# Feed-forward weights in 8 KB runs per partition, read back by transposes of every fourth column

## The chip, the cores and the metric

One core of one Trainium2 chip runs the whole program. The metric is the device time of one execution in microseconds; lower is better. The kernel before was run three times, and one more execution was profiled. TensorE (PE) multiplies, with its weight loads shown apart (PEld); VectorE (DVE), ScalarE (ACT) and GpSimd (POOL) work on tiles; SyncE (SP) only issues DMAs, which 16 DMA engines carry out.

## What is computed

The reference is a two-layer backbone over 1024 tokens of width 1024: layer 0 mixes the tokens with a gated DeltaNet and pooling, layer 1 with a short gated convolution, and each layer ends with a mixture of 16 experts in which every expert chooses its 128 tokens. The change touches that part alone:

```python
aff = softmax(h @ router)                        # (n, 16)
gate, idx = top_k(aff.T, cap)                    # cap = 2 * 1024 / 16 = 128 tokens per expert
xg = h[idx]                                      # (16, 128, 1024)
hid = silu(xg @ w_gate) * (xg @ w_up)            # w_gate, w_up: (16, 1024, 512)
y = (hid @ w_down) * gate[..., None]             # w_down: (16, 512, 1024)
out = zeros_like(h).at[idx].add(y)
```

All arrays are float32.

## The kernel before

A product of full precision is made of three TensorE products: both operands are split into a high part (fp32r) and a rest, and high by high, high by low and low by high are summed (`mm3`, lines 140 to 142). So each granule of weights, 1 MB in 128 partitions of 2048 floats, goes through three steps. SyncE fetches it into one of eight `raw` buffers (line 71), ScalarE casts it to `whi` (line 88, in one piece in these stages), and VectorE subtracts to `wlo` (line 89), which frees the raw buffer for the next fetch. The split buffers `whi` and `wlo` come from a rotation of several pools; a cast waits until TensorE has read what was there.

`granules` (line 380) gives the order in which an expert's weights are fetched: gate and up of the first 512 input rows, gate and up of the other 512, then two granules of `w_down`, each with all 512 rows and half of the columns. In DRAM a row of each granule is 512 floats, and partition p takes rows p, 128 + p, 256 + p and 384 + p: four runs of 2 KB. `fetch`, `prefetch` and `weight` keep fetched and split granules in order, some ahead of their use.

`experts` (line 405) is the loop over the 16 experts. For each it gathers the rows of the expert three places later (`gather`: GpSimd's indirect DMA, line 359, after counts on ScalarE and TensorE, lines 353 and 354; ScalarE then copies the affinity out of the gathered rows, line 362). It transposes the next expert's rows, eight TensorE transposes of 128 columns each into two PSUM tiles (`transposed`, line 372), and splits the results into `xh` and `xl`. Then come 48 gate and up products of 512 columns, Silu on ScalarE (line 434), the product with up on VectorE (line 435), four transposes of the hidden values (line 438) and their split into `hh` and `hl`. The down projection has 16 products with `hh` (line 452), granule after granule, and 8 with `hl` (line 455), four per granule, after each four of which VectorE scales a half of `y` out of PSUM (line 457). GpSimd adds `y` to the tokens' rows by an indirect DMA (line 462); the last expert's rows are added by one-hot products in `sums`.

In a transpose the data is the operand that TensorE loads as weights, and the identity matrix streams through.

The tile framework orders each engine's instructions by a schedule of its own when the kernel is built, with the marks `high_priority` and `issue_after`; within an engine they then run in that order. The loads of `ada_w` early in the program and in layer 1 use other helpers, which the change does not touch; a part of them has 8 KB per partition in one run.

Of the kernel before, what the change touches and what calls it, by code (L numbers as in the profile page):

```python
# [9 lines left out]
F32 = mybir.dt.float32  # L10
# [10 lines left out]
P = 128  # L21
D = 1024
# [4 lines left out]
NE = 16  # L27
# [7 lines left out]
class Cycle:  # L35
# [6 lines left out]
    def next(self):  # L42
        self.at += 1
        return self.pools[(self.at - 1) % len(self.pools)]
# [15 lines left out]
class Weights:  # L60
# [6 lines left out]
    def fetch(self, src, shape):  # L67

        t = self.raw.tile([P, self.size], F32, tag="raw", name=self.co.name("raw"))[:, : math.prod(shape)]
        t = t.rearrange("p (a b) -> p a b", a=shape[0])  # L70
        self.loaded = self.co.nc.sync.dma_start(t, src).ins
        return t
# [131 lines left out]
    nc.vector.memset(co.ones16, 1.0)  # L204


class Moe:


# [155 lines left out]
    def transposed(self, xg, pool, ps):  # L365

        co = self.co
        halves = []
        for half in range(2):
            pt = ps.tile([P, 512], F32, tag="tr", name=co.name("pt"))  # L370
            for k in range(4):
                self.nc.tensor.transpose(
                    pt[:, k * P : (k + 1) * P], xg[:, (4 * half + k) * P : (4 * half + k + 1) * P], co.ident
                )
            hi, lo = (pool.tile([P, 4, P], F32R, tag=tag, name=co.name(tag), bufs=3) for tag in ("xh", "xl"))
            co.split(hi.rearrange("p k t -> p (k t)"), lo.rearrange("p k t -> p (k t)"), pt)
            halves.append((hi, lo))
        return halves

    def granules(self):  # L380

        w_gate, w_up, w_down = self.w
        for e in range(NE):
            for half in range(2):
                for w in (w_gate, w_up):
                    yield w[e, half * 512 : (half + 1) * 512, :].rearrange("(k p) f -> p k f", p=P)
            for half in range(2):
                yield w_down[e, :, half * 512 : (half + 1) * 512].rearrange("(k p) f -> p k f", p=P)

    def fetch(self, weights, n):  # L390
        for _ in range(n):
            self.fetched.append(weights.fetch(next(self.stream), (4, 512)))

    def prefetch(self, weights, n, lo_engine=None, in_raw=False):
        for _ in range(n):
# [9 lines left out]
    def experts(self, pool, weights, ps, raws, before_last, scatter_last):  # L405

        co, nc = self.co, self.nc
        rows = [self.gather(e, pool, ps) for e in range(3)]
        ahead = self.transposed(rows[0][2], pool, ps)
        with co.tc.issue_after(self.routed):
            self.prefetch(weights, min(4, 6 - len(self.ahead)), nc.gpsimd)
        with co.tc.issue_after(self.placed):
            self.prefetch(weights, 6 - len(self.ahead), nc.vector)
        for e in range(NE):
            (idx, aff, _), halves = rows.pop(0), ahead
            if e + 3 < NE:  # L420
                rows.append(self.gather(e + 3, pool, ps))
            if rows:
                with co.tc.high_priority(100):
                    ahead = self.transposed(rows[0][2], pool, ps)
            lo_engine = nc.vector if e == NE - 1 else None
            acts = [ps.tile([P, 512], F32, tag="gu", name=co.name("gu")) for w in range(2)]
            for half, (hi, lo) in enumerate(halves):
                for pa in acts:
                    g = self.weight(weights, lo_engine)
                    for k in range(4):  # L430
                        co.mm3(pa, (hi[:, k, :], lo[:, k, :]), (g[0][:, k, :], g[1][:, k, :]), half == k == 0, half == 1 and k == 3)
            with co.tc.high_priority(100):
                sg = pool.tile([P, DE], F32, tag="sg", name=co.name("sg"), bufs=1)
                nc.scalar.activation(sg, acts[0], AF.Silu)
                nc.vector.tensor_tensor(sg, sg, acts[1], op=ALU.mult)
                pt = ps.tile([P, 512], F32, tag="tr", name=co.name("pt"))
                for k in range(4):
                    nc.tensor.transpose(pt[:, k * P : (k + 1) * P], sg[:, k * P : (k + 1) * P], co.ident)
                hh = pool.tile([P, 4, P], F32R, tag="hh", name=co.name("hh"), bufs=1)
                hl = pool.tile([P, 4, P], F32R, tag="hl", name=co.name("hl"), bufs=1)  # L440
                co.split(hh.rearrange("p k t -> p (k t)"), hl.rearrange("p k t -> p (k t)"), pt)

            y = (
                pool.tile([P, ROW], F32, tag="xg", name=co.name("y"), bufs=3)[:, :D]
                if e == NE - 2 else pool.tile([P, D], F32, tag="y", name=co.name("y"), bufs=1)
            )
            down = [(self.weight(weights, lo_engine, e == NE - 1), ps.tile([P, 512], F32, tag="y", name=co.name("py"))) for half in range(2)]

            for g, py in down:
                for k in range(4):  # L450
                    for w in range(2):
                        nc.tensor.matmul(py, hh[:, k, :], g[w][:, k, :], start=k == w == 0, stop=False)  # L452
            for half, (g, py) in enumerate(down):
                for k in range(4):
                    nc.tensor.matmul(py, hl[:, k, :], g[0][:, k, :], start=False, stop=k == 3)  # L455
                sl = slice(half * 512, (half + 1) * 512)
                nc.vector.scalar_tensor_tensor(y[:, sl], py, aff, self.g2[:, sl], op0=ALU.mult, op1=ALU.mult)  # L457
            if e == NE - 1:
                xs = self.sums(idx, y, raws, pool, ps, *before_last(pool, ps))
                if not scatter_last:  # L460
                    return xs
            self.scattered = nc.gpsimd.indirect_dma_start(  # L462
                out=self.acc[:, :],
                out_offset=bass.IndirectOffsetOnAxis(ap=idx, axis=0),
                in_=y,
                in_offset=None,
                compute_op=ALU.add,
            ).ins
        return xs
# [1035 lines left out]
def hybrid_dit_kernel(stack, tc, aps):  # L1505
# [29 lines left out]
    with ExitStack() as sa:  # L1535
# [21 lines left out]
        with ExitStack() as left:  # L1557
# [40 lines left out]
            with tc.issue_after(loads[5]):  # L1598
                gs = {0: [weights.split(raw) for raw in fetch(0)]}
# [13 lines left out]
        invert = lambda h: mx.invert(h, E[h], Ys, heads, ps)  # L1613
        weave(project(0, 0))
        ahead = fetch(1)
        weave(project(0, 1), mx.decays(0, E[0], heads))
        base = []
        for h in range(H):

            gs[h + 1] = [weights.split(ahead.pop(0))]  # L1620
            weave(project(h, 2), front(h, 0), base[-3:])
            gs[h + 1] += [weights.split(raw) for raw in ahead]
            before = invert(h - 1) if h else []
            if h == H - 1:
                ada_pools.close()
                blocks = left.enter_context(pooled("base"))
                Ys += mx.inverse_buffers(blocks, 2)
            base = front(h, 2) + urgent(mx.base(h, heads if h < H - 1 else blocks, heads, nc.vector if h == H - 1 else nc.gpsimd), 300)
            if h + 1 < H:
                weave(project(h + 1, 0), front(h, 1), before[:8], ada[h][:18])  # L1630
                ahead = fetch(h + 2)
                weave(
                    project(h + 1, 1), base[:-3], before[8:] + mx.decays(h + 1, E[h + 1], heads), ada[h][18:],
                )
# [297 lines left out]
```

## Time and profile before

| what | value |
|---|---|
| median of 3 runs | 1886.85 us (1879.98 to 1890.77) |
| the profiled execution | 1879.51 us, of it span from first to last instruction 1877.7 us |
| TensorE's busy share of the span | 88% |
| VectorE, ScalarE, GpSimd | 70%, 48%, 28% |
| DMA | 443.71 MB, 236 GB/s over the span |
| mean granted TensorE clock | 0.929 of full speed |
| feed-forward stage of layer 0, experts | 730 to 1070 us |
| feed-forward stage of layer 1, experts | 1530 to 1850 us |

The profile gives an engine's busy time, not its use: products are pipelined, and a busy TensorE may still wait between products. The share of DMA is the time that packets took over 16 engines; two queues whose packets overlap on an engine can bring it over 1. The chain of waits follows the work back from the last instruction, at each step to what released it; "issue" in it is time in which an engine waited for nothing that the profile shows. A line of the profile is a line of the kernel; line 71 is every fetch of weights, lines 88 and 89 every split, lines 140 to 142 every product of three.

### The profile page before, as it was taken

What the parts mean: (1) busy time and instruction counts of PE and PEld (TensorE: products, weight loads), DVE (VectorE), ACT (ScalarE), POOL (GpSimd) and SP (SyncE); (2) the same over time, 40 slices, a digit from 0 to 9 for tenths busy, and PEclk for the clock granted to TensorE, in tenths of its full rate; (3) what the DMA queues carried; (4) which work ended last, traced back from release to release, by engine and by line L of the source; (5) the groups of instructions that cost most, each with busy time, mean ns of one, the idle gap of its engine ahead of it and who ended that gap; (6) DMA issues with size and microseconds to landing.
All of it is one profiled execution on the core that took longest, in us unless ns stands there. A gap on an engine that the chain in (4) does not pass through costs nothing.

```text
span 1877.7 us, 26055 instructions
## 1 busy us (share of the span) xinstructions
PE 1655.3 (88%) x9561; PEld 1344.1 (72%) x9561; DVE 1305.4 (70%) x1975; ACT 897.3 (48%) x1570; POOL 530.7 (28%) x549
## 2 busy tenths in 40 slices
PE   6999997979969963999898999999999559989995
PEld 2988775758868752877677677888888447867873
DVE  4637776567878884888878858433545558888896
ACT  3645332434742434878766451101122358778673
POOL 4310386571340352212121261000012412122222
PEclk7999998879989985999999999999999769999998
DMA  7426764659667964899999648423264549999995
GB/s 289 146 81 193 222 207 125 174 157 278 194 243 259 386 252 146 302 346 372 367 345 329 206 144 301 147 68 113 73 225 142 181 138 327 373 360 353 373 326 192
DMA packets 261397, 443.71 MB, mean 236 GB/s; under 512 B 46521, under 2 KB 108714, under 8 KB 257174
## 3 DMA queue, kind: packets, MB, share of 16 engines
q1 hardware_dynamic: 252198, 408.76, 62.9%
q0 software_dynamic: 9072, 33.30, 7.0%
q8 instruction: 75, 1.23, 0.3%
q14 instruction: 52, 0.43, 0.1%
HBM read 368.65 MB, written 73.35 MB: 235 GB/s over the span
## 4 chain that ended last, share of the span: by engine, by line
PE 50%; DVE 13%; DMA 7%; ACT 5%; issue 4%; SPq 2%; POOL 0%; DVEq 0%; ACTq 0%; POOLq 0%
PE py L452 5%; PE gu L141 4%; PE gu L140 4%; PE gu L142 4%; PE pin L140 4%; PE pin L141 4%; PE pin L142 4%; PE po L141 3%; PE po L142 3%; PE po L140 3%; DVE wlo L89 3%; ACT whi L88 3%; PE py L455 2%; DMA raw<-in_w_up_dram 2%; SPq L918 1%
## 5 line engine op out<-in xcount | busy, mean ns | idle before, releaser
L89 DVE TENSOR_TENSOR wlo<-raw,whi 128x2048 fp32r<-128x2048 f32 (+3 forms) x245 | 471.9, 1959 | 82.6 <-ACT whi L88 82.5
L88 ACT CAST whi<-raw 128x2048 fp32r<-128x2048 f32 (+3 forms) x271 | 420.9, 1598 | 213.5 <-PE pin L141 77.7
L140 PE MATMUL gu<-whi,xh 128*128 128x512 f32 x512 | 206.3, 407 | 13.3 <-ACT whi L88 12.4
L141 PE MATMUL gu<-wlo,xh 128*128 128x512 f32 x512 | 207.4, 406 | 6.2 <-DVE wlo L89 6.2
L142 PE MATMUL gu<-whi,xl 128*128 128x512 f32 x512 | 204.4, 403 | 0.8 <-DVE xl L135 0.8
L462 POOL DMA_INDIRECT acc<-y,idx x31 | 83.9, 2708 | 356.8 <-DVE y L457 340.9
L141 PE MATMUL pin<-h1T,whi 128*128 128x512 f32 x384 | 150.4, 393 | 0.0
L142 PE MATMUL pin<-h1T,wlo 128*128 128x512 f32 x384 | 150.0, 393 | 0.0
L140 PE MATMUL pin<-h1T,whi 128*128 128x512 f32 x384 | 149.3, 398 | 0.0
L89 POOL TENSOR_TENSOR wlo<-raw,whi 128x1024 fp32r<-128x1024 f32 (+2 forms) x26 | 80.6, 3117 | 167.1 <-ACT whi L88 167.0
L140 PEld LDWEIGHTS gu<-whi,xh 128*128 128x128 f32 x512 | 98.7, 193 | 37.8 <-ACT whi L88 14.0
L141 PEld LDWEIGHTS gu<-wlo,xh 128*128 128x128 f32 x512 | 98.6, 193 | 31.0 <-DVE wlo L89 8.8
L142 PEld LDWEIGHTS gu<-whi,xl 128*128 128x128 f32 x512 | 98.1, 192 | 23.1 <-DVE xl L135 1.1
L452 PE MATMUL py<-whi,hh 128*128 128x512 f32 x256 | 106.4, 419 | 8.1 <-ACT hh L134 8.0
L788 DVE SCALAR_TENSOR_TENSOR adsum<-raw,cs,adsum 128x512 f32<-128x512 f32 (+1 forms) x77 | 95.3, 1238 | 24.9 <-DMA raw<-in_ada_w_dram 24.4
L452 PE MATMUL py<-wlo,hh 128*128 128x512 f32 x256 | 105.1, 412 | 0.0
L353 ACT ACTIVATE oh<-places,aff 128x128 f16<-128x128 f16 x256 | 77.9, 394 | 46.9 <-DVE aff L342 46.9
L140 PE MATMUL pq<-hT,whi 128*128 128x512 f32 (+1 forms) x256 | 98.0, 383 | 1.6 <-ACT last L1082 1.0
L359 POOL DMA_INDIRECT xg<-table,idx x32 | 48.8, 1526 | 175.9 <-ACT idx L357 133.1
L142 PE MATMUL pq<-hT,wlo 128*128 128x512 f32 (+1 forms) x256 | 97.6, 381 | 0.0
L141 PE MATMUL pq<-hT,whi 128*128 128x512 f32 (+1 forms) x256 | 97.6, 381 | 0.0
L141 PE MATMUL po<-wlo,mh 128*128 128x512 f32 x224 | 90.4, 403 | 4.5 <-DVE wlo L89 4.5
(387 smaller groups left out, 3744.3 us busy)
## 6 DMA issues: line engine op xcount, KB each, us to landing
raw<-in_w_gate_dram SPq DMA_DIRECT2D x64, 1024.0 KB
raw<-in_w_up_dram SPq DMA_DIRECT2D x64, 1024.0 KB
raw<-in_w_down_dram SPq DMA_DIRECT2D x64, 1024.0 KB
raw<-in_ada_w_dram SPq DMA_DIRECT2D x32, 1024.0 KB
raw<-in_ada_w_dram SPq DMA_DIRECT2D x64, 256.0 KB
raw<-in_sc_w_in_dram SPq DMA_DIRECT2D x12, 1024.0 KB
table<-h SPq DMA_DIRECT2D x16, 520.0 KB
raw<-in_ev_w_in_dram SPq DMA_DIRECT2D x16, 512.0 KB
```

The source lines that it names most:

```text
L88: nc.scalar.copy(hi[:, part], raw[:, part])
L89: (lo_engine or e).tensor_sub(lo[:, part], raw[:, part], hi[:, part])
L140: nc.tensor.matmul(out, lhs[0], rhs[0], start=start, stop=False)
L141: nc.tensor.matmul(out, lhs[0], rhs[1], start=False, stop=False)
L142: nc.tensor.matmul(out, lhs[1], rhs[0], start=False, stop=stop)
L353: nc.scalar.activation(oh[:, t, :], co.places, AF.Sign, bias=self.before[:, t, e : e + 1])
L359: nc.gpsimd.indirect_dma_start(out=xg, out_offset=None, in_=self.table[:, :], in_offset=bass.IndirectOffsetOnAxis(ap=idx, axis=0))
L452: nc.tensor.matmul(py, hh[:, k, :], g[w][:, k, :], start=k == w == 0, stop=False)
L455: nc.tensor.matmul(py, hl[:, k, :], g[0][:, k, :], start=False, stop=k == 3)
L462: self.scattered = nc.gpsimd.indirect_dma_start(out=self.acc[:, :], out_offset=bass.IndirectOffsetOnAxis(ap=idx, axis=0), in_=y, in_offset ...
L788: nc.vector.scalar_tensor_tensor(st["sum"], raw, cs[:, k, 0:1], st["sum"], op0=ALU.mult, op1=ALU.add)
L918: mx.nc.sync.dma_start(dst, src)
```

## The change

The weights of a granule are laid out so that partition p holds neighbouring rows of DRAM: for gate and up rows 4p to 4p + 3 of the 512, for `w_down` rows 2p and 2p + 1 of 256 rows with all 1024 columns. Each partition's part is then one run of 8 KB. The products sum over partitions, so the other operand has to have the same rows in the same partitions: the transposes of the gathered rows read every fourth column of a half, those of the hidden values every second column of a half (`every`). The down projection goes over k (the four sets of 128 hidden rows), both parts of the split and both halves of the columns, with the two PSUM tiles in turn, and the last eight products over both granules for each half. The bytes, the splits and the number of products are as before.

```diff
--- before.py
+++ after.py
@@ -202,6 +202,11 @@
     nc.vector.memset(co.one16, 1.0)
     co.ones16 = c.tile([P, 1], F16, name="ones16")
     nc.vector.memset(co.ones16, 1.0)
+
+
+def every(x, n, k):
+
+    return x.rearrange("p (t k) -> p k t", k=n)[:, k, :]
 
 
 class Moe:
@@ -370,7 +375,7 @@
             pt = ps.tile([P, 512], F32, tag="tr", name=co.name("pt"))
             for k in range(4):
                 self.nc.tensor.transpose(
-                    pt[:, k * P : (k + 1) * P], xg[:, (4 * half + k) * P : (4 * half + k + 1) * P], co.ident
+                    pt[:, k * P : (k + 1) * P], every(xg[:, 4 * half * P : 4 * (half + 1) * P], 4, k), co.ident
                 )
             hi, lo = (pool.tile([P, 4, P], F32R, tag=tag, name=co.name(tag), bufs=3) for tag in ("xh", "xl"))
             co.split(hi.rearrange("p k t -> p (k t)"), lo.rearrange("p k t -> p (k t)"), pt)
@@ -383,13 +388,13 @@
         for e in range(NE):
             for half in range(2):
                 for w in (w_gate, w_up):
-                    yield w[e, half * 512 : (half + 1) * 512, :].rearrange("(k p) f -> p k f", p=P)
+                    yield w[e, half * 512 : (half + 1) * 512, :].rearrange("(p k) f -> p k f", p=P), (4, 512)
             for half in range(2):
-                yield w_down[e, :, half * 512 : (half + 1) * 512].rearrange("(k p) f -> p k f", p=P)
+                yield w_down[e, half * 256 : (half + 1) * 256, :].rearrange("(p k) f -> p k f", p=P), (2, D)
 
     def fetch(self, weights, n):
         for _ in range(n):
-            self.fetched.append(weights.fetch(next(self.stream), (4, 512)))
+            self.fetched.append(weights.fetch(*next(self.stream)))
 
     def prefetch(self, weights, n, lo_engine=None, in_raw=False):
         for _ in range(n):
@@ -435,7 +440,8 @@
                 nc.vector.tensor_tensor(sg, sg, acts[1], op=ALU.mult)
                 pt = ps.tile([P, 512], F32, tag="tr", name=co.name("pt"))
                 for k in range(4):
-                    nc.tensor.transpose(pt[:, k * P : (k + 1) * P], sg[:, k * P : (k + 1) * P], co.ident)
+                    half = sg[:, k // 2 * 256 : (k // 2 + 1) * 256]
+                    nc.tensor.transpose(pt[:, k * P : (k + 1) * P], every(half, 2, k % 2), co.ident)
                 hh = pool.tile([P, 4, P], F32R, tag="hh", name=co.name("hh"), bufs=1)
                 hl = pool.tile([P, 4, P], F32R, tag="hl", name=co.name("hl"), bufs=1)
                 co.split(hh.rearrange("p k t -> p (k t)"), hl.rearrange("p k t -> p (k t)"), pt)
@@ -444,15 +450,17 @@
                 pool.tile([P, ROW], F32, tag="xg", name=co.name("y"), bufs=3)[:, :D]
                 if e == NE - 2 else pool.tile([P, D], F32, tag="y", name=co.name("y"), bufs=1)
             )
-            down = [(self.weight(weights, lo_engine, e == NE - 1), ps.tile([P, 512], F32, tag="y", name=co.name("py"))) for half in range(2)]
-
-            for g, py in down:
+            down = [self.weight(weights, lo_engine, e == NE - 1) for half in range(2)]
+            pys = [ps.tile([P, 512], F32, tag="y", name=co.name("py")) for half in range(2)]
+            part = lambda k, w, half: down[k // 2][w][:, k % 2, half * 512 : (half + 1) * 512]
+
+            for k in range(4):
+                for w in range(2):
+                    for half, py in enumerate(pys):
+                        nc.tensor.matmul(py, hh[:, k, :], part(k, w, half), start=k == w == 0, stop=False)
+            for half, py in enumerate(pys):
                 for k in range(4):
-                    for w in range(2):
-                        nc.tensor.matmul(py, hh[:, k, :], g[w][:, k, :], start=k == w == 0, stop=False)
-            for half, (g, py) in enumerate(down):
-                for k in range(4):
-                    nc.tensor.matmul(py, hl[:, k, :], g[0][:, k, :], start=False, stop=k == 3)
+                    nc.tensor.matmul(py, hl[:, k, :], part(k, 0, half), start=False, stop=k == 3)
                 sl = slice(half * 512, (half + 1) * 512)
                 nc.vector.scalar_tensor_tensor(y[:, sl], py, aff, self.g2[:, sl], op0=ALU.mult, op1=ALU.mult)
             if e == NE - 1:
```

## Rows read from the trace of the kernel before

**Rows 1.** The page, busy time, share of the span and instructions of TensorE

```profile
PE 1655.3 (88%) x9561; PEld 1344.1 (72%) x9561; DVE 1305.4 (70%) x1975; ACT 897.3 (48%) x1570; POOL 530.7 (28%) x549
```

**Rows 2.** Table by stage: PE, PEld, DVE, ACT, POOL busy us, clock, DMA share, GB/s

```profile
730.00:1070.00 340.00, 313.67 (x1477) 248.90 (x1478) 266.68 (x195) 243.12 (x319) 66.14 (x35) 0.95 0.91 308
...
1530.00:1850.00 320.00, 305.03 (x1448) 243.75 (x1446) 262.41 (x190) 230.90 (x279) 69.78 (x30) 0.97 0.93 320
```

**Rows 3.** Line 434 in each stage: count, duration in ns, first and last start

```profile
L434 ACT ACTIVATE sg<-gu x16: 581/598/610, 756.2 to 1049.7; 128x512 f32<-128x512 f32 x16
...
L434 ACT ACTIVATE sg<-gu x16: 579/598/616, 1545.1 to 1833.4; 128x512 f32<-128x512 f32 x16
```

**Rows 4.** Chain in order of time, 855 to 1005 us: start, duration, what

```profile
856.55 0.35 PE pi L354 x8
...
906.17 0.87 PE pt L372 x8
907.05 3.75 PE py L452 x16
910.80 1.88 PE py L455 x8
```

**Rows 5.** DMA queues, 1700 to 1780 us: packets, MB, share of 16 engines

```profile
q1 hardware_dynamic: 12444, 24.71, 83.0%
q0 software_dynamic: 1272, 4.66, 21.3%
```

**Rows 6.** DMA queues, 1136 to 1140 us, then 1125 to 1133 us

```profile
DMA packets 186, 1.39 MB, mean 348 GB/s; under 512 B 16, under 2 KB 16, under 8 KB 16
...
q1 hardware_dynamic: 186, 1.39, 85.8%
...
q1 hardware_dynamic: 352, 2.62, 88.0%
```

**Rows 7.** Chain by line, 740 to 1070 us, then 1530 to 1850 us

```profile
by line: PE py L452 14.2%; PE gu L140 11.6%; PE gu L141 11.4%; PE gu L142 11.2%; issue 9.1%; ACT whi L88 7.9%; DMA raw<-in_w_up_dram 6.7%; DVE wlo L89 5.5%; PE py L455 4.3%; DMA raw<-in_w_gate_dram 3.2%; DMA xg<-table,idx 2.9%; PE pt L372 2
...
by line: PE py L452 16.9%; PE gu L141 13.4%; PE gu L142 13.2%; PE gu L140 13.0%; ACT whi L88 7.1%; DVE wlo L89 6.8%; issue 6.1%; PE py L455 5.3%; DMA raw<-in_w_gate_dram 3.3%; PE pt L372 3.3%; DMA xg<-table,idx 3.1%; DMA raw<-in_w_up_dram 2
```

**Rows 8.** Waits of TensorE, 780 to 860 us, then 1580 to 1660: us, times, longest

```profile
PE gu L141 <- DVE wlo L89: 1.6, 3, 0.7
...
PE gu L141 <- DVE wlo L89: 4.2, 3, 3.0
PE gu L140 <- ACT whi L88: 0.9, 1, 0.9
```

**Rows 9.** Waits, ScalarE's casts for split buffers, each stage

```profile
ACT whi L88 <- PE py L455: 8.0, 8, 2.7
...
ACT whi L88 <- PE py L455: 5.0, 6, 1.5
```

**Rows 10.** Waits, ScalarE for gathered rows, each stage

```profile
ACT aff L362 <- DMA xg<-table,idx: 10.4, 4, 4.1
...
ACT aff L362 <- DMA xg<-table,idx: 10.7, 5, 3.2
```

**Rows 11.** Single lines: duration in ns, min, median, max (the last: busy us, mean ns)

```profile
L372 PEld LDWEIGHTS pt<-ident,xg x256: 137/141/231, 740.4 to 1811.1; 128*128 128x128 f32 x128
...
L1268 DVE COPY base<-base x4: 1049/1078/1110, 274.6 to 453.6; 104x1024 f32<-104x1024 f32 x4
...
L1023 ACT ACTIVATE g_beta<-gates x1: 344/344/344, 111.5 to 111.5; 128x80 f32<-128x80 f32 x1
...
L1026 ACT ACTIVATE g_e<-g_u x1: 254/254/254, 111.8 to 111.8; 128x80 f32<-128x80 f32 x1
...
L1024 DVE TENSOR_TENSOR g_u<-gates,gate_par x1: 293/293/293, 110.0 to 110.0; 128x80 f32<-128x80 f32 x1
...
L1031 DVE TENSOR_TENSOR g_ld<-g_u,gate_par x1: 242/242/242, 115.5 to 115.5; 128x80 f32<-128x80 f32 x1
...
L89 DVE TENSOR_TENSOR wlo<-raw,whi 128x2048 fp32r<-128x2048 f32 x90 | 202.8, 2288 | 27.1 <-ACT whi L88 27.0
```

## The prediction

> **What bounds the kernel now.** The page comes first: TensorE is busy 88% of the span [rows 1], but that average says nothing of the two stretches that the change touches, the feed-forward stages. So the table by stage is read next [rows 2]: from 730 to 1070 us and from 1530 to 1850 us the DMA engines are 0.91 and 0.93 busy and TensorE, VectorE and ScalarE work beside them most of the time. No engine stands out, so each is costed per expert. Sixteen experts run in a stage, and their Silu instructions mark the pace [rows 3]: from the first to the last, (1049.7 - 756.2) / 15 = 19.57 us per expert in layer 0 and (1833.4 - 1545.1) / 15 = 19.22 us in layer 1.
>
> TensorE's own work per expert, from dense places of the chain [rows 4]: 16 + 8 down products (3.75 + 1.88, 0.235 each), 48 gate and up products of the same form (11.3), 12 transposes (0.87 / 8 each, 1.3), 8 one-column counts (0.35): 18.6 us. So TensorE loses 0.97 and 0.62 us per expert, (0.97 + 0.62) x 15 = 24 us in both stages together. That is the most that a perfect feed of weights could give inside them.
>
> DMA per expert: one queue carries the weights, the other the gathers and scatters. From 1700 to 1780 us [rows 5] the weights' queue spends 0.830 x 16 x 80 / 24.71 = 43.0 us of one engine per MB, that is 88 ns for each 2 KB packet; an expert's six granules (6.29 MB) take 43.0 x 6.29 / 16 = 16.9 us. The other queue adds 0.213 x 80 = 17.0 us in that stretch of 4.2 experts, 4.1 us each. Together 21.0 us, of which some overlaps (the shares sum to 1.05), so about 20: DMA is slightly slower than the 19.2 to 19.6 us at which experts pass, and lives on the granules fetched ahead. It is the tightest supplier, by a small margin over TensorE.
>
> **The change, part by part.**
>
> *Packets of 8 KB.* The same bytes go in a quarter of the packets. ScalarE's and VectorE's splits of a granule keep their size. The kernel already has 8 KB packets, in the loads of ada_w: from 1136 to 1140 us, where only 16 of 186 packets are shorter, the queue needs 0.858 x 16 x 4 / 1.39 = 39.5 us per MB, 324 ns a packet; from 1125 to 1133 us it is 0.880 x 16 x 8 / 2.62 = 43.0 [rows 6], as for 2 KB, because starting transfers are in it. I take 39.5, the fuller stretch: 8% less, 1.4 us of 16.9 per expert, and keep 0 as the other end. DMA's pace becomes about 20.0 - 1.3 = 18.7 us per expert, beside TensorE's 18.6: it no longer sets the pace alone.
>
> What that is worth is read from the waits, not from DMA's busy time. In the chain, landings of raw weights hold 6.7 + 3.2% of 340 us in layer 0 and 3.3 + 2% of 320 us in layer 1 [rows 7]: 34 + 17 = 51 us, and 8% of it is 4.1 us. Seen from TensorE, in the two stretches where those landings stand (780 to 860, 1580 to 1660 us) it waits for splits 1.6 + 4.2 + 0.9 = 6.7 us [rows 8]. The two agree; I take 6.5 us gained, with ends 0 and 24 (all that TensorE loses).
>
> *Down projection by rows.* The 24 products stay, and so does the order of need: the first eight read only the first granule (k = 0, 1), as before. What moves is when a split buffer comes free. Before, the first granule's high part was last read by the first half's four L455 products; now both halves read both granules, and it is free after the sixth of the eight: two products, 0.47 us, later. ScalarE's casts wait for exactly this, 8 + 6 times [rows 9]. Behind those casts the rest of ScalarE's queue stands, and TensorE waits for them. At most 14 x 0.47 = 6.6 us; TensorE's own waits for casts in such places are a handful, so I take five, 2.4 us lost, ends 0 and 6.6. VectorE's evacuation of y keeps its place.
>
> *Transposes of every fourth and every second column.* 8 of 12 transposes per expert read gathered rows 16 bytes apart, 4 read the hidden values 8 bytes apart. The data is the operand of the weight load, which takes 141 ns (median) for 128 contiguous columns [rows 11]. No strided read by TensorE is in this trace. The nearest rows are of other engines [rows 11]: VectorE's copy with its source 128 bytes apart takes 1078 ns for 1024 elements, 1.05 ns each, while its subtraction of contiguous columns takes 2288 ns for 2048, 1.12 ns each; that speaks for no cost. ScalarE's activation with its source 64 bytes apart takes 344 ns for 80 elements where the contiguous one takes 254: 1.1 ns more each. VectorE's addition beside it takes 293 against 242 ns. By VectorE's copy the cost is 0; by ScalarE's it is 128 x 1.1 = 144 ns for a load, and 256 transposes of fourth columns make 37 us. A gain is excluded: the load reads as many elements. I take 0, because the copy is the longest of these rows and its rate is not hidden in fixed cost, and keep 37 us as the end. The stride of 8 bytes I cost at nothing; 128 transposes at half that price would be 9 us.
>
> [...]
>
> *Sum.* -6.5 + 2.4 + 0 = -4 us. The profiled execution took 1879.5 us (span 1877.7), at the lower edge of the three runs shown, whose median is 1886.85. Four microseconds less is 1875.5 for an execution like the profiled one, and 1883 for the median, which I forecast.
>
> **Rivals.**
>
> *B, slower: weight loads of every fourth column are slow.* Place: the eight L372 loads of each expert. Four transposes follow one another at 0.11 us, less than one load's 141 ns, so a longer load cannot hide within the four; it decides as soon as it adds some 50 ns (256 x 50 ns = 13 us). Price by ScalarE's row: 37 us of TensorE, which holds 55% of the chain in layer 0 and 65% in layer 1 [rows 7], so 0.6 x 37 = 22 us, less the 4 gained: +18, 1905. For it: ScalarE's row, and a TensorE with 0.6 to 1.0 us per expert to spare. Against: VectorE's copy. Chance 0.28.
>
> *C, clearly faster: the whole loss of TensorE goes.* If weights come early enough, ScalarE and VectorE find their splits ready and work ahead, and most of the 24 us goes: 19 us less, 1868. For it: DMA is at 1.05 of its engines in the second half of both stages. Against: only 6.7 us of TensorE's waits stand where landings do; the others follow ScalarE's casts that wait for TensorE itself [rows 9], and VectorE has 267 us of work in 340 [rows 2]. It also needs strided loads at no cost. Chance 0.22.
>
> *D, slower: gathers and scatters stand behind longer packets.* A gather has 128 rows, 8 per engine. If each takes turns with a weight packet, it waits 8 x (324 - 88) ns = 1.9 us longer. ScalarE already waits for 9 of the 32 gathers, 21.1 us in all [rows 10]; 9 x 1.9 = 17 us, less the 4 gained: +13, 1900. It decides only where ScalarE arrives before the rows do; the other 23 have slack. Chance 0.08.
>
> *A, the forecast:* chance 0.42. If packets of 8 KB are no faster than 43.0 us per MB, the change does not do what it is for, and the time stays within A as well.
>
> **How the numbers follow.** About 0.5%, 9.4 us, is what a measurement of this kernel can tell from no change. A lies within it, C below, B and D above: faster 0.22, same 0.42, slower 0.36. The range goes down to C with nearly all 24 us (1863) and up to B with 0.6 of 37 and the 6.6 of the split buffers, little gained (1886.85 + 22 + 6.6, 1914 rounded down): beyond it lie strides that cost still more, and gains outside the experts. A's own range is 1878 to 1896, no change give or take 9 us.
>
> **What would show it.** Right: the weights' queue near 39.5 us per MB; L372's loads still near 141 ns and four of them in 0.44 us; fewer landings of raw in the chain; Silu to Silu 19.0 to 19.5 us. B: L372's loads far over 141 ns. C: under 18.9 us per expert. D: ScalarE's wait for xg over 21.1 us. I am wrong if the split buffers, not the feed, prove to hold ScalarE back: then casts waiting for L455 would grow well past 13 us.

## The result: 0.8% slower, and the profile after

The changed kernel takes 1903.79 us (median of five executions, 1891.63 to 1909.49), the kernel before 1886.85 us beside it: ratio 1.0086 (95% interval 1.0061 to 1.0112, in brackets below). Run once more beside other kernels it gave 1.0072 [1.0053, 1.0091]. Both lie within the forecast range and above the 1883 us that were forecast. The profiled execution took 1891.63 us (span 1889.7), the shortest of its five; the repeat's took 1896.86 (span 1895.1).

The rate of the weights' queue became what was forecast. First the page, then the table by stage, then the DMA queues from 1700 to 1780 us (packets, MB, share of 16 engines), all of the kernel after:

```profile
PE 1665.4 (88%) x9561; PEld 1358.7 (72%) x9561; DVE 1305.2 (69%) x1975; ACT 896.8 (47%) x1570; POOL 534.2 (28%) x549
...
DMA packets 187669, 443.71 MB, mean 235 GB/s; under 512 B 46521, under 2 KB 108714, under 8 KB 158870
```

```profile
730.00:1070.00 340.00, 315.93 (x1492) 253.53 (x1492) 265.47 (x199) 241.75 (x319) 70.96 (x35) 0.95 0.85 305
1530.00:1850.00 320.00, 300.25 (x1418) 242.45 (x1419) 257.65 (x182) 235.73 (x301) 67.33 (x31) 0.96 0.89 324
```

```profile
q1 hardware_dynamic: 3375, 24.52, 75.2%
q0 software_dynamic: 1152, 4.23, 20.7%
```

The weights' queue now needs 0.752 x 16 x 80 / 24.52 = 39.3 us per MB where it needed 43.0 [rows 5]; 39.5 was forecast. DMA's share of the two stages falls from 0.91 and 0.93 [rows 2] to 0.85 and 0.89. The feed is lighter, and yet the experts pass more slowly. Silu's line shows it, first of the profiled kernel after, then of the repeat (count, duration in ns, first and last start):

```profile
L439 ACT ACTIVATE sg<-gu x16: 578/599/607, 760.1 to 1054.7; 128x512 f32<-128x512 f32 x16
...
L439 ACT ACTIVATE sg<-gu x16: 585/598/610, 1550.7 to 1845.4; 128x512 f32<-128x512 f32 x16
```

```profile
L439 ACT ACTIVATE sg<-gu x16: 587/599/608, 760.6 to 1056.7; 128x512 f32<-128x512 f32 x16
...
L439 ACT ACTIVATE sg<-gu x16: 580/598/606, 1553.5 to 1851.2; 128x512 f32<-128x512 f32 x16
```

Between the first and the last Silu lie 294.6 + 294.7 = 589.3 us, in the repeat 296.1 + 297.7 = 593.8, where the kernel before has 293.5 + 288.3 = 581.8 [rows 3]: 7.5 and 12 us more, most of them in layer 1. In layer 0 the count is not quite of the same work: the changed kernel issues one expert's 16 products with `hh` (3.8 us) ahead of the last Silu, the kernel before behind it. Measured to VectorE's last addition of a one-hot product (line 503, then 511), the two stages take 326.3 and 318.9 us before, 329.3 and 325.2 after, 332.4 and 327.9 in the repeat: two executions of one kernel differ by some 3 us a stage. Another 4 us of each span's difference stand ahead of the first Silu, where the two programs are the same up to the gathers; the profiled execution of before was a quick one (1879.51 us against a median of 1886.85).

Where did the lighter feed go? The chain by line of the kernel after, 740 to 1070 and 1530 to 1850 us:

```profile
by line: PE py L460 12.9%; PE gu L140 12.6%; PE gu L142 12.1%; PE gu L141 12.0%; ACT whi L88 9.9%; issue 8.5%; DMA xg<-table,idx 4.5%; DMA acc<-y,idx 4.4%; PE py L463 3.8%; DVE wlo L89 3.8%; PE pt L377 3.4%; DMA raw<-in_w_up_dram 3.1%; DMA 
...
by line: PE py L460 15.6%; PE gu L141 15.1%; PE gu L140 14.6%; PE gu L142 14.4%; issue 6.8%; PE py L463 5.6%; DVE wlo L89 5.2%; ACT whi L88 4.9%; DMA xg<-table,idx 3.8%; PE pt L377 3.5%; DMA raw<-in_w_down_dram 2.7%; ACT oh L358 2.4%; PE pt
```

Landings of raw weights, 51 us of the two chains before [rows 7], hold 28 us now: 3.1% of 330 and 2.7% of 320 us in these rows, and 9.4 us for `w_gate` in layer 0, where the row is cut off. Gathers (xg) grew from 2.9 and 3.1% to 4.5 and 3.8%: from 19.5 to 27 us. The scatter's 4.4% (acc) was not in the chain before; it stands at the end of layer 0. ScalarE's waits tell the same (730 to 1070 us, then 1530 to 1850: us in total, times, longest):

```profile
ACT aff L367 <- DMA xg<-table,idx: 13.0, 6, 5.5
ACT whi L88 <- PE py L463: 7.6, 2, 6.8
...
ACT whi L88 <- DMA raw<-in_w_up_dram: 1.8, 1, 1.8
...
ACT aff L367 <- DMA xg<-table,idx: 13.5, 4, 6.5
...
ACT whi L88 <- PE py L463: 7.6, 7, 1.9
ACT whi L88 <- DMA raw<-in_w_up_dram: 1.3, 1, 1.3
```

For gathers it waits 26.5 us (28.5 in the repeat) where it waited 21.1 [rows 10], and the longest waits are 5.5 and 6.5 us where they were 4.1 and 3.2. For split buffers it waits 15.2 where it waited 13.0 [rows 9]. These two are the suspects.

The gathers themselves land later. Median time from issue to landing, 790 to 1040 us, for the kernel before, for one with gate and up alone in 8 KB runs (`packets_stride4` below), and for the kernel after:

```profile
DMA to landing us min/median/max: 7.0/7.8/9.3
```

```profile
DMA to landing us min/median/max: 7.2/9.0/11.5
```

```profile
DMA to landing us min/median/max: 8.4/10.2/11.1
```

With more of the weights in long packets, the other queue's rows land later: 7.8, 9.0, 10.2 us. In the second stage it is 8.2, 8.9 and 9.8. The medians scatter: with all weights in 2 KB packets they are 7.8 and 8.5 us in the first stage and 8.2 twice in the second (before, `before_strided`), with all in 8 KB 10.2 to 10.6 and 9.6 to 10.3 (after, `after_repeat`, `after_contiguous`, `after_late_copy`); those between are 8.9 to 9.4 and 7.9 to 9.6, the latter overlapping both. The delay is as large as rival D had it, 1.6 to 2.4 us here where 1.9 was worked out from 324 and 88 ns a packet. That a gathered row takes turns with a weight packet was D's assumption: the landings agree with its estimate, and the turns themselves no run shows.

TensorE's clock is a third suspect. Over the executions beside `after_repeat` the mean granted clock was 0.921 of full speed in the changed kernel and 0.926 before; 0.005 of 1902 us is 9.5 us, an estimate of the most that this can be worth. The extra time does not start there: between the first and the last Silu the profiled execution of after was granted 0.97 and 0.98 in the two layers, just as the kernel before, and was 7.5 us longer. The repeat's profiled execution was granted 0.920 over its span where the one of after had 0.924, and there the clock may have added to the loss.

### The profile page after: what moved, and what is told of

Its sections match the earlier page's. It is cut to its first block, busy times and chain, and to the rows that moved or that the text cites. A ratio compares the mean times of both kernels' runs of the same rounds, so it can differ in the third digit from the quotient of the medians.

```text
span 1889.7 us, 26060 instructions
## 1 busy us (share of the span) xinstructions
PE 1665.4 (88%) x9561; PEld 1358.7 (72%) x9561; DVE 1305.2 (69%) x1975; ACT 896.8 (47%) x1570; POOL 534.2 (28%) x549
## 4 chain that ended last, share of the span: by engine, by line
PE 51%; DVE 11%; DMA 7%; ACT 5%; issue 5%; SPq 1%; POOL 1%; DVEq 0%; ACTq 0%; POOLq 0%
PE py L460 5%; PE gu L140 5%; PE gu L141 5%; PE gu L142 5%; PE pin L140 4%; PE pin L141 4%; PE pin L142 4%; PE po L141 3%; PE po L142 3%; PE po L140 3%; ACT whi L88 3%; DVE wlo L89 2%; PE py L463 2%; DMA xg<-table,idx 1%; DVE junk L306 1%
## 5 line engine op out<-in xcount | busy, mean ns | idle before, releaser
L470 POOL DMA_INDIRECT acc<-y,idx x31 | 89.3, 2879 | 350.6 <-DVE y L465 350.2
L460 PE MATMUL py<-whi,hh 128*128 128x512 f32 x256 | 88.2, 423 | 8.2 <-ACT hh L134 8.2
L140 PE MATMUL po<-whi,mh 128*128 128x512 f32 x224 | 91.2, 408 | 0.0
```

Source lines behind the costliest of these rows:

```text
L140: nc.tensor.matmul(out, lhs[0], rhs[0], start=start, stop=False)
L460: nc.tensor.matmul(py, hh[:, k, :], part(k, w, half), start=k == w == 0, stop=False)
L470: self.scattered = nc.gpsimd.indirect_dma_start(out=self.acc[:, :], out_offset=bass.IndirectOffsetOnAxis(ap=idx, axis=0), in_=y, in_offset ...
```

## The experiments

Theory G: ScalarE's queue stands at the one-column copy of the affinity (L367, L362 before), which waits for the gather; longer packets let the gather land later, and this eats the packets' gain. Theory R: the down projection by rows frees the first granule's high part later, and ScalarE's casts and all behind them wait. Theory O: neither, but the order of instructions that the scheduler makes of the change; in the traces some 420 of TensorE's 9,561 products and transposes stand elsewhere. Rival S: strided loads. Except where told, kernels that are compared issue in the same order on every engine. The first four share one set of runs of before, and so do the next four, and the four after them.

| kernel | ratio to before | median, us |
|---|---|---|
| packets_only | 0.9995 [0.9974, 1.0017] | 1885.88 |
| before_strided | 0.9999 [0.9974, 1.0024] | 1887.01 |
| down_by_rows_only | 1.0030 [1.0014, 1.0047] | 1892.67 |
| after_contiguous | 1.0064 [1.0041, 1.0088] | 1900.22 |
| before_late_copy | 1.0027 [1.0010, 1.0044] | 1891.85 |
| packets_stride4_late_copy | 0.9992 [0.9973, 1.0011] | 1887.29 |
| after_late_copy | 1.0016 [1.0001, 1.0031] | 1890.51 |
| after_early_release | 1.0042 [1.0025, 1.0059] | 1895.43 |
| after_repeat | 1.0072 [1.0053, 1.0091] | 1901.57 |
| packets_stride4 | 1.0015 [0.9995, 1.0034] | 1889.36 |
| down_by_rows_late_copy | 1.0011 [0.9993, 1.0028] | 1889.05 |
| after_late_and_release | 1.0026 [1.0011, 1.0040] | 1892.07 |
| down_by_rows_early_release | 1.0004 [0.9986, 1.0022] | 1888.49 |
| before_late_release | 1.0054 [1.0033, 1.0076] | 1900.87 |

### The three parts alone

**packets_only**: into the kernel before,

```diff
-                    yield w[e, half * 512 : (half + 1) * 512, :].rearrange("(k p) f -> p k f", p=P)
+                    yield w[e, half * 512 : (half + 1) * 512, :].rearrange("(p k) f -> p k f", p=P)
```

> The kernel before with gate and up fetched in runs of 8 KB per partition and nothing else changed: transposes contiguous, w_down in runs of 2 KB, every engine's order that of the kernel before. (Rows of weights and of tokens no longer belong together; sizes and work are the same.) Packets theory: gathers land after 9 to 10 us instead of 8.2, ScalarE waits 24 to 27 us for them instead of 21, slower by 2 to 6 us, ratio 1.001 to 1.003. Feed theory (mine of the prediction): weights come faster and TensorE waits less, 4 to 6 us gained, 0.996 to 0.998. Order and strides theories: 1.000 within 0.002.

**before_strided**: both strided transposes in the kernel before, packets of 2 KB.

```diff
-                    pt[:, k * P : (k + 1) * P], xg[:, (4 * half + k) * P : (4 * half + k + 1) * P], co.ident
+                    pt[:, k * P : (k + 1) * P], every(xg[:, 4 * half * P : 4 * (half + 1) * P], 4, k), co.ident
...
-                    nc.tensor.transpose(pt[:, k * P : (k + 1) * P], sg[:, k * P : (k + 1) * P], co.ident)
+                    half = sg[:, k // 2 * 256 : (k // 2 + 1) * 256]
+                    nc.tensor.transpose(pt[:, k * P : (k + 1) * P], every(half, 2, k % 2), co.ident)
```

> The kernel before with nothing changed but the transposes, which read every fourth and every second column; packets stay at 2 KB and the down projection is as before. (The rows of hidden values and of weights no longer belong together; sizes and work are the same.) Strides theory: slower by most of the 16 us, ratio 1.006 to 1.010. Order theory and packets theory: 384 x 12 ns = 4.6 us at most, 1.000 to 1.003.

**down_by_rows_only**: the kernel after with contiguous transposes and

```diff
-                    yield w[e, half * 512 : (half + 1) * 512, :].rearrange("(p k) f -> p k f", p=P), (4, 512)
+                    yield w[e, half * 512 : (half + 1) * 512, :].rearrange("(k p) f -> p k f", p=P), (4, 512)
...
-                yield w_down[e, half * 256 : (half + 1) * 256, :].rearrange("(p k) f -> p k f", p=P), (2, D)
+                yield w_down[e, half * 256 : (half + 1) * 256, :].rearrange("(k p) f -> p k f", p=P), (2, D)
```

> The changed kernel with contiguous transposes and without 8 KB packets: gate and up in runs of 2 KB as before, w_down by 256 rows of 1024 columns in runs of 4 KB. The output is the reference's. ScalarE's, VectorE's, TensorE's and GpSimd's orders are those of the changed kernel. Order theory: slower by 8 to 13 us, ratio 1.004 to 1.007, with gaps of TensorE behind ScalarE's casts as in the changed kernel. Packets theory: the gathers land after 8.2 us (median) again, ScalarE waits about 21 us for them, ratio 0.998 to 1.002. Strides theory: 0.998 to 1.002.

**after_contiguous**: the kernel after with its 8 KB packets and contiguous transposes.

```diff
-                    pt[:, k * P : (k + 1) * P], every(xg[:, 4 * half * P : 4 * (half + 1) * P], 4, k), co.ident
+                    pt[:, k * P : (k + 1) * P], xg[:, (4 * half + k) * P : (4 * half + k + 1) * P], co.ident
...
-                    nc.tensor.transpose(pt[:, k * P : (k + 1) * P], every(half, 2, k % 2), co.ident)
+                    nc.tensor.transpose(pt[:, k * P : (k + 1) * P], sg[:, k * P : (k + 1) * P], co.ident)
```

> The changed kernel with its transposes reading contiguous columns again; every engine's order is that of the changed kernel and the packets stay at 8 KB. (The rows that a transpose gives no longer belong to the rows of weights they are multiplied with; sizes and work are the same.) Strides theory: in the changed kernel's trace a strided transpose follows the one before after 120 ns where the contiguous one took 109, and its weight load takes 205 to 209 ns instead of 141; if that is the whole loss, this run is back at the time of the kernel before, ratio 0.995 to 1.002. Order theory (the down projection by rows changed the order and the release of split buffers): it stays slow, 1.005 to 1.008, since 384 transposes x 12 ns are only 4.6 us of the 16. Packets theory (gathers and scatters stand behind 8 KB packets): it stays slow too, with ScalarE's wait for gathered rows still near 26 us.

Packets alone and strides alone change nothing that can be measured: 0.9995 is neither the gain of the prediction nor the loss of the packets theory. The down projection by rows alone costs 0.30%, less than the order theory expected. On top of it the packets cost another 0.34% (1.0064 against 1.0030), though in the order of before they cost nothing. Strides on top of that: from 1.0064 to 1.0072 or 1.0086, inside the intervals. So rival S does not decide, and the strides' loads show why. In the kernel after, 730 to 1850 us:

```profile
L377 PEld LDWEIGHTS pt<-ident,xg x256: 195/209/230, 744.1 to 1823.1; 128*128 128x128 f32 x128
L444 PEld LDWEIGHTS pt<-ident,sg x124: 194/205/226, 767.6 to 1842.4; 128*128 128x128 f32 x124
```

A load takes 209 or 205 ns where a contiguous one takes 141 [rows 11]. But four transposes in the chain take, after and then before (start, duration, what):

```profile
1606.96 0.47 PE pt L377 x4
```

```profile
1596.56 0.44 PE pt L372 x4
```

0.03 us more for four where the loads are 64 to 68 ns longer each: most of the longer load is hidden, and 96 such fours make some 3 us.

### The late copy: theory G

The copy of the affinity goes behind the two casts of the same rows' transposes; the rest stays.

```diff
         nc = self.nc
-        nc.scalar.copy(hi, src)
+        self.last_cast = nc.scalar.copy(hi, src).ins
...
-        nc.scalar.copy(aff, xg[:, D + e : D + e + 1])
-        return idx, aff, xg
+        return idx, aff, xg, e
...
             halves.append((hi, lo))
+        with co.tc.issue_after(co.last_cast):
+            co.nc.scalar.copy(aff, xg[:, D + e : D + e + 1])
         return halves
```

**before_late_copy**: this in the kernel before.

> The kernel before, with ScalarE's one-column copy of the affinity moved behind the two casts of the same expert's transposed rows, where the gather has long landed. Theory G (ScalarE's queue stands at gathers, and that costs time): the 21.1 us that ScalarE waits for xg become under 3, and the time falls by 5 to 15 us (ratio 0.992 to 0.997). Theory R (the gather's wait is slack, the order of the down products sets the loss): ScalarE waits as long for something else, ratio 0.998 to 1.002.

**packets_stride4_late_copy**: this, gate and up in 8 KB runs, and transposes of every fourth column, in the kernel before.

> The kernel before with gate and up weights in 8 KB runs, transposes of every fourth column, the down projection as before, and the late copy; every engine issues in the same order as in the kernel before with the late copy. Theory G: with no wait at gathers the packets' gain of landings is kept, the strided loads cost 256 x 12 ns = 3 us at most; ratio to before 0.988 to 0.996, and 2 to 6 us below the kernel before with the late copy. Theory R: ratio 0.998 to 1.003, and the same as the kernel before with the late copy.

**after_late_copy**: this in the kernel after.

> The changed kernel with the same late copy. Theory G: the 26.5 us of waits for xg go and with them what the longer packets cost; the change keeps only its strides and its order, ratio to before 1.000 to 1.005. Theory R: the waits were slack, ratio stays 1.007 to 1.011.

**down_by_rows_late_copy**: this in `down_by_rows_only`.

> The changed kernel with 2 KB packets for gate and up, w_down by rows in 4 KB runs, contiguous transposes, and the late copy: every engine issues as in the changed kernel with the late copy, so the two differ by packets and strides alone. Theory G: without the wait at gathers, packets no longer cost; this kernel is as slow as the changed one with the late copy or slower, ratio 1.001 to 1.005. If packets and strides cost something that has nothing to do with gathers, as they did together in this order with the early copy (0.56%), it is faster by that: 0.996 to 0.999.

**packets_stride4**: packets and fourth columns in the kernel before, with the early copy.

> The kernel before with gate and up weights in 8 KB runs and transposes of every fourth column, and nothing else: order as before, down projection as before, early copy. Each of the two alone measured 0.9995 and 0.9999. Theory G: ScalarE waits 23 to 28 us for xg where it waited 21, and the gain of landings is given back; ratio 0.998 to 1.002. If the two parts add up to more than their sum, as strides did on top of packets in the order of the changed kernel, 1.002 to 1.005.

**after_repeat**: the kernel after, unaltered.

> The changed kernel once more, unaltered, beside the next three: its first comparison rests on five executions that lie 18 us apart, and its profiled one was the fastest of them. If that comparison holds, the ratio is again 1.006 to 1.011, and a more typical profiled execution shows where it is slow: theory G expects more than the 26.5 us of ScalarE's waits for xg, theory R more than the 15.2 us of casts that wait for L463. If the first comparison was a poor draw, the ratio is 1.002 to 1.005.

Each pair below issues in one order, so only packets and strides differ in it (in the order of before those of gate and up and the fourth columns; in the others all of them, w_down from 4 to 8 KB). The third row's kernels are those of the next section:

| | 2 KB, contiguous | 8 KB, strided | difference |
|---|---|---|---|
| order of before, early copy | 1 | 1.0015 | +0.15% |
| order of before, late copy | 1.0027 | 0.9992 | -0.35% |
| order of after, early copy | 1.0030 | 1.0072 | +0.42% |
| order of after, early release, early copy | 1.0004 | 1.0042 | +0.38% |
| order of after, late copy | 1.0011 | 1.0016 | +0.05% |

The same edit costs more where ScalarE's copy is early than where it is late: 0.50% apart in the order of before and 0.37% in that of after, about 7 to 9 us, with intervals of about 0.35% on either. The late copy moves some 300 of TensorE's other instructions too. The early release of the next section moves as many and leaves the packets' cost as it was (0.38%), so it is not any change of order that takes the cost away; that it is the copy itself is the likeliest reading, and no run moves the copy alone. In the order of before and with the copy late the packets bring 0.35%, 6.6 us (interval about 0.25%), the gain that the prediction had counted. ScalarE's waits in `after_late_copy`, 1530 to 1850 us:

```profile
ACT xh L134 <- PE pt L377: 25.6, 11, 6.7
ACT hh L134 <- PE pt L446: 13.2, 6, 5.2
ACT sg L441 <- PE gu L142: 13.1, 5, 6.2
ACT whi L88 <- PE py L465: 9.4, 8, 2.7
...
ACT whi L88 <- DMA raw<-in_w_up_dram: 1.2, 1, 1.2
```

No wait for a gather is left, though gathers still take 10.6 and 10.3 us to land here. What theory G had wrong is the kernel before: it loses its 21 us of such waits too, and is 0.27% slower, not faster, outside what either theory expected. Its loss is in one layer: from the first Silu to the last one-hot addition layer 0 takes 322.6 us (326.3 in before) and layer 1 330.5 (318.9). Why layer 1 loses is open, and so is what the waits cost in the kernel before. Nor is a wait for gathered rows a loss by itself: `packets_only` waits as long as the kernel after, 26.0 us, and measured 0.9995.

```profile
ACT aff L362 <- DMA xg<-table,idx: 15.0, 4, 8.4
...
ACT aff L362 <- DMA xg<-table,idx: 11.0, 5, 3.4
```

### The release of the split buffers: theory R

**after_early_release**: the last eight products of the kernel after, both halves' k = 0, 1 first.

```diff
             for half, py in enumerate(pys):
-                for k in range(4):
+                for k in range(2):
+                    nc.tensor.matmul(py, hl[:, k, :], part(k, 0, half), start=False, stop=False)
+            for half, py in enumerate(pys):
+                for k in range(2, 4):
                     nc.tensor.matmul(py, hl[:, k, :], part(k, 0, half), start=False, stop=k == 3)
```

> The changed kernel with its last eight down products reordered: both halves' k = 0, 1 first, then k = 2, 3, so that the first granule's high part is free after the fourth product and not the sixth; the first half of y comes two products later. Theory R: ScalarE's casts that wait for these products find their buffer 0.47 us earlier, ratio to before 1.005 to 1.007. Theory G, and the theory that the evacuation of y matters: no gain, ratio 1.008 to 1.011.

**down_by_rows_early_release**: the same edit in `down_by_rows_only`. In both kernels some 300 of TensorE's instructions move with it, and the two issue alike.

> The kernel with the down projection by rows alone (2 KB packets for gate and up, w_down in 4 KB runs, contiguous transposes, early copy; 1.0030), with its last eight products reordered so that the first granule's high part is free after the fourth. Theory R (the late release costs the 0.30%): back to 0.998 to 1.001. Theory O (the order of the instructions in the two stages costs it, whatever the release): 1.002 to 1.005, or any other value, since this edit too moves some instructions.

**before_late_release**: the opposite in the kernel before; some 220 move.

```diff
+            for k in range(2):
+                nc.tensor.matmul(down[1][1], hl[:, k, :], down[1][0][0][:, k, :], start=False, stop=False)
             for half, (g, py) in enumerate(down):
-                for k in range(4):
+                for k in range(2 * half, 4):
                     nc.tensor.matmul(py, hl[:, k, :], g[0][:, k, :], start=False, stop=k == 3)
```

> The kernel before with two of the second half's last products ahead of the first half's, so that the first granule's high part is free after the sixth of the eight and not the fourth, as in the change. Theory R: 1.002 to 1.004, and ScalarE's casts wait more than 13 us for L455. Theory O: 0.998 to 1.002 unless the few moved instructions happen to matter, and those waits stay near 13 us.

**after_late_and_release**: the late copy and the early release in the kernel after.

> The changed kernel with the late copy and with the early release of the first granule's high part together. Alone they measured 1.0016 and 1.0042 where the changed kernel measured 1.0086. If the two free different waits they add up: 0.996 to 0.999, a kernel faster than both. If both only let ScalarE run past the same few places: 1.000 to 1.003.

All three edits go the way of theory R: with the early release the down projection by rows returns from 1.0030 to 1.0004, and the kernel after from 1.0072 and 1.0086 to 1.0042; the late release costs the kernel before 0.54%, more than theory R expected. In each, the first half of y comes two products later, so it is not its evacuation. ScalarE's casts, first stage, then second: in `before_late_release` (L457 is the line of those products), then in `down_by_rows_early_release`, then in `down_by_rows_only`:

```profile
ACT whi L88 <- PE py L457: 9.8, 7, 3.2
...
ACT whi L88 <- PE py L457: 10.9, 6, 4.8
```

```profile
ACT whi L88 <- PE py L463: 7.5, 8, 2.7
...
ACT whi L88 <- PE py L463: 4.7, 6, 1.5
```

```profile
ACT whi L88 <- PE py L463: 7.3, 2, 6.7
...
ACT whi L88 <- PE py L463: 6.3, 6, 1.9
```

With the late release 13 casts wait 20.7 us where 14 waited 13.0 [rows 9]: 7.7 us more. With the early one it is 12.2 us in 14, with the same longest of 2.7 and 1.5. But in `down_by_rows_only`, which loses 0.30%, 8 casts wait 13.6 us, hardly more than before, and in the kernel after 9 wait 15.2: these waits do not show the loss.

Nor do the three edits change the release alone. It moves alike in both layers, but the order of the other instructions does not. In `before_late_release` some 200 of TensorE's moved instructions are in layer 1 and 25 in layer 0, and the loss is in layer 1: from the first to the last Silu, 294.3 and 301.8 us where the kernel before has 293.5 and 288.3 [rows 3].

```profile
L434 ACT ACTIVATE sg<-gu x16: 578/598/605, 764.5 to 1058.8; 128x512 f32<-128x512 f32 x16
...
L434 ACT ACTIVATE sg<-gu x16: 580/594/617, 1553.5 to 1855.3; 128x512 f32<-128x512 f32 x16
```

The early release moves some 240 in layer 0 and 60 in layer 1. Between `down_by_rows_only` and its early release, first Silu to last one-hot addition, layer 0 falls from 331.2 to 322.7 us and layer 1 from 323.0 to 321.2. So in the layer whose order stays nearly as it was, the release is worth little: the late one changes layer 0 from 326.3 to 326.0 us, though its casts wait 9.8 us there instead of 8.0, and the early one takes 1.8 us off layer 1, both within the 3 us between executions. What costs the 0.30% is the down projection by rows; whether by its release (R) or by the order that comes with it (O) these runs do not settle, and the layers speak for O.

Early release and late copy do not add up (1.0026): that kernel's order differs from `after_late_copy`'s in some 350 instructions of TensorE, and why it is not the fastest is open. No kernel here beats the one before by more than its interval.

## Why the prediction was wrong

**Packets, -6.5: the step that failed.** The rate was right (39.3 us per MB against 39.5), and landings in the chain fell by far more than 8%, from 51 to 28 us. What failed is "I take 6.5 us gained": it took the waits that the feed ends as time won, and left out what would be late next. Packets alone measured 0.9995. With the early copy packets and strides bring +0.15% in the order of before and +0.42% in the change's, +3 and +8 us; the forecast gain shows only with the late copy in the order of before, -0.35%.

**Rival D, put at 0.08, named the likeliest next thing.** Its delay was right (1.9 us each; 1.6 to 2.4 measured), and its sign, over 21.1 us of waits for xg, came with 26.5 and 28.5 us. Its sum was not: 9 x 1.9 = 17 us of waits were forecast and 5 to 7 came, and that its end (1900) lies near 1903.79 is luck, for the down projection's 5.7 us are not in it. Nor does the sign decide: `packets_only` shows it too, with 26.0 us, and loses nothing. What D lacked is the rest of ScalarE's queue: "the other 23 have slack" counts gathers and not the work that stands behind a waiting one, and by the pairs the price goes with an early copy or a late one.

**Down projection by rows, +2.4: mis-sized, its mechanism not shown.** Alone it measured +0.30%, 5.7 us, within its ends of 0 and 6.6. The prediction put it down to the later release; a release just as late measured +0.54%, 10 us, in the kernel before, beyond the ends, but in the one layer where the order moved too. The order of the other instructions was no term of the sum. The sign for which the prediction would call itself wrong, casts growing well past 13 us, came as 15.2 in the kernel after and 13.6 with this part alone: not clearly.

**Strides, 0: right in the time, wrong in the reason.** They do load more slowly, by 68 ns, over the 50 ns at which rival B was to decide. The step "a longer load cannot hide within the four" is refuted by 0.47 against 0.44 us. The row of ScalarE from which B was priced compares two functions, Sigmoid and Abs, and not the stride alone. The loads of second columns, which the prediction costed at nothing, take nearly as long as those of fourth columns: 205 ns beside 209.

**Rival C** fell with the first step. **The sum**, -6.5 + 2.4 + 0, reads +8 (packets and strides, early copy, in this order) + 5.7 = +13.7 us as measured. It meets the 13.6 us of the repeat (0.72% of 1887) because the 8 was taken from it; the first comparison has 16.2 (0.86%). Two slips changed nothing: the shares of layer 0's chain are of 330 us, not 340, and the range's upper end adds up to 1915, not 1914.

## What to carry to other kernels

When a transfer is made cheaper by longer packets (here from 43.0 to 39.3 us per MB), look at the small transfers of the other queue first: here they landed 1.6 to 2.4 us later, and ScalarE stood at them for 26.5 us where it had stood for 21.1, with work behind them in its queue that has nothing to do with them. Try the instruction that waits for a small transfer where its data is used, and measure: here it took 0.6 to 0.7% off the changed kernel and cost the kernel before 0.27%. When the loops of a product are exchanged, follow the last reader of every buffer, and compare the order of all engines as well: edits that moved two products of 0.235 us in every expert changed the time by 5 to 10 us, and moved some 200 to 300 other instructions of TensorE with them. Where an edit moves instructions in one layer and hardly any in the other, compare the two layers.

## What the runs showed of the hardware that was not expected

TensorE's weight load of 128 columns of float32 takes 141 ns contiguous, 205 ns with columns 8 bytes apart and 209 ns with 16 bytes, yet four chained transposes take 0.47 us against 0.44. A gather of 128 rows beside the weights' queue lands after 7.8 and 8.5 us (medians of the first stage) where all weights come in 2 KB packets and after 10.2 to 10.6 us where all come in 8 KB packets.
